# Neighbourhood attention of a one-core hybrid block: scores computed in two layouts, or in one with the exponentials transposed

## The chip, the core and the metric

One core of a Trainium2 chip runs the whole layer in one launch. Time is the device time of that core in microseconds (us). All matrix operands are 32-bit: a product of full precision is written as two or three passes of `float32r` halves (a rounded high part and the remainder as a low part), so most operands exist as a pair `..h`, `..l`.

## The reference

```python
xn = rms_norm(x, norm_g) * (1 + sc_x) + sh_x          # 1024 positions x 1024, modulated by c
cn = rms_norm(ctx, norm_g) * (1 + sc_c) + sh_c        # 256 context positions
f_in, f_gate, q, k, v, na_gate = split(xn @ w_in)     # the context needs only k, v
q, k, kc = rms_norm per head (8 heads of 64)
f_out  = real(fft2(f_in)) @ w_four * silu(f_gate)
s_loc  = where(in window of 8 rows x 16 columns, q.k / 8 + rel_bias, -1e30)
s_ctx  = q.kc / 8                                     # all 256 context keys
p      = softmax(concat(s_loc, s_ctx))                # one softmax over both
na_out = (p_loc @ v + p_ctx @ vc) * silu(na_gate)
out    = x + g_x * (concat(f_out, na_out) @ w_out)
```

Positions are stored by blocks of 8 grid columns, so a block `t` of 128 queries sees keys of the blocks `t-1`, `t`, `t+1` and the two blocks of the context: 512 keys for the first and last block, 640 for the others.

## The kernel before

The layer runs in four stretches. Up to about 140 us: conditioning, norm, the Fourier gate and the Fourier group. From there to about 210 us: Fourier output, projections of the context and the first part of the query, key and value projections. From about 211 us to 538 us: attention, four pairs of heads `p`, two heads `h` in a pair, with projections between its steps. Then the output projection (`of`, L1625).

**Two passes over the scores.** Attention does the following for each head.

- The row pass, `row_max` (L1153), eight times, once for a block `t` of 128 queries: TensorE makes scores `s` with queries on the partitions and keys along the row (L1166, L1168; two passes for the halves). VectorE adds the bias, negates, writes the row to `pr` and takes the row's extreme into `tr` (L1173). ScalarE takes the exponential of `pr` in place, with the extreme as bias, and accumulates the sum of the row (L1177). Of this pass only the extremes and the sums are used: `pr` has two buffers and is overwritten.
- `end_rows` (L1198): one transposition brings extremes and reciprocal sums to eight rows (`pm`). GpSimd spreads the extremes (`spread`, L1188, tile `mrow`) into the free half of the query operand `qs2`, where the ones in `ks2` add them to every score of the second pass, and the reciprocals into `rexp` (two tiles).
- The column pass, `scores` (L1234), twelve steps: TensorE makes the same scores again with keys on the partitions and up to four query blocks side by side (`st`, L1250 and L1251). A step on the window adds a transposed bias on VectorE (`e`, L1259, from `biast`, 448 KB a head) and takes the exponential on ScalarE (L1269). A context step takes it straight from PSUM (L1267). ScalarE rounds `e` to `eh` (L209), and VectorE or GpSimd makes the remainder `el` (L204; GpSimd mostly at context steps). TensorE multiplies both with the values into `pv` (L1282, L1283, L1287).

The pair ends in `finish` (L1296): reciprocals are multiplied into the gate, and the gate into the output.

**What sets the order.** Engines execute in order. Their order is made in Python by a planner: coroutines (`seq_rows`, `seq_scores`, `seq_products` and others) each put out their next piece as soon as the planned clock `now` and the flags in `done` allow it, and each piece on ScalarE, VectorE and GpSimd has a planned duration (`a_t`, `d_t`, `p_t`). When none can go on, `run_fill` puts a product of the projections on TensorE: `pqkv` (L801), `png` (L823) and, in the last pair, the Fourier half of the output projection `po` (L1446). These need nothing from the attention step in progress and are called the filler below. PSUM has one tile `s` of two banks, two tiles `pv0` and `pv1`, two banks for the filler and two (`tb`, counted in `tbs`) that the column pass shares with the transpositions of queries and keys.

## Time and profile before

| what | value |
|---|---|
| median of 3 runs | 602.2 us (601.92 to 603.22) |
| the profiled execution | 599.94 us, its span 598.2 us |
| TensorE busy | 548.5 us, 92% of the span |
| VectorE busy | 468.6 us, 78% |
| ScalarE busy | 354.4 us, 59% |
| GpSimd busy | 222.7 us, 37% |
| chain that ended last, by engine | TensorE 59%, VectorE 24%, ScalarE 6%, issue 5% |

PE is TensorE, PEld its loads of weights, DVE VectorE, ACT ScalarE, POOL GpSimd. "Busy" counts an instruction from start to end. On TensorE matmuls overlap in the pipeline: a matmul over 384 columns lasts 0.34 us in the rows, and the next one starts 0.17 us after it. What a matmul costs is the distance from start to start, called its cadence below.

### The profile page before, as it was taken

The numbers are of one execution on the slowest core, as the hardware profiler recorded it, in microseconds if no ns is written. First come the engines' busy times: TensorE is split into PE (matmuls) and PEld (weight loads), VectorE is DVE, ScalarE is ACT, GpSimd is POOL, SyncE is SP. The second block draws the span as 40 slices with busy tenths as digits, with TensorE's granted clock in tenths as the row PEclk, the third lists the DMA queues.
The fourth block names the chain that finished last, engine by engine and source line by source line (L and its number), as shares of the span: only waits on it lengthen the run. The fifth ranks groups of instructions, "written<-read, shape, count | busy, mean of one in ns | idle before, by whom it ended". The sixth has DMA issues, their size and how long they took to land.

```text
span 598.2 us, 8590 instructions
## 1 busy us (share of the span) xinstructions
PE 548.5 (92%) x2923; PEld 481.6 (81%) x2923; DVE 468.6 (78%) x904; ACT 354.4 (59%) x747; POOL 222.7 (37%) x198
## 2 busy tenths in 40 slices
PE   6799567999999999979999999999999799999997
PEld 4588457989778979979889889799898578787886
DVE  5999999976897787677895878976779959779342
ACT  6865053365633586856877878878677747654100
POOL 3100004015653545342545533444544836424200
PEclk9999958999999999989999999999999898999999
DMA  8970524026783422121032030331104563113152
GB/s 334 407 284 2 175 70 142 2 85 200 260 261 112 149 76 59 43 62 46 22 102 85 22 89 1 111 84 36 50 2 163 163 232 112 66 61 119 35 193 89
DMA packets 42889, 68.83 MB, mean 115 GB/s; under 512 B 3542, under 2 KB 25430, under 8 KB 42844
## 3 DMA queue, kind: packets, MB, share of 16 engines
q1 hardware_dynamic: 41836, 64.60, 32.2%
q0 software_dynamic: 1008, 3.67, 1.8%
q8 instruction: 23, 0.38, 0.3%
q14 instruction: 22, 0.18, 0.1%
HBM read 59.35 MB, written 8.91 MB: 114 GB/s over the span
## 4 chain that ended last, share of the span: by engine, by line
PE 59%; DVE 24%; ACT 6%; issue 5%; DMA 3%; POOL 2%; SPq 1%; DVEq 0%; POOLq 0%; ACTq 0%
PE pqkv L801 16%; PE of L1625 7%; PE pg L369 5%; PE po L1446 5%; PE pv L1287 4%; DVE junk L251 4%; PE png L823 3%; PE st L1250 3%; PE st L1251 3%; PE s L1166 2%; PE s L1168 2%; DVE pr L1173 2%; DVE el L204 2%; DVE l L530 2%; DVE ks L895 1%
## 5 line engine op out<-in xcount | busy, mean ns | idle before, releaser
L801 PE MATMUL pqkv<-wh,xnh 128*128 128x384 f32 x256 | 87.2, 341 | 0.0
L801 PE MATMUL pqkv<-wl,xnh 128*128 128x384 f32 x256 | 87.1, 340 | 0.0
L801 PE MATMUL pqkv<-wh,xnl 128*128 128x384 f32 x256 | 86.8, 339 | 0.0
L1173 DVE CUSTOM_DVE_ANT_0 pr<-s,bias 128x640 f32<-128x640 f32 (+1 forms) x64 | 50.5, 788 | 22.5 <-PE s L1168 16.4
L1177 ACT ACTIVATE pr<-pr,tr 128x640 f32<-128x640 f32 (+1 forms) x64 | 51.4, 803 | 27.4 <-DVE tr L1173 27.2
L707 POOL TENSOR_TENSOR hrs<-hss,mhalf 128x4 f32<-128x4 f32 (+1 forms) x34 | 38.5, 1135 | 65.0 <-DVE hss L704 57.3
L204 DVE TENSOR_TENSOR el<-e,eh 128x384 fp32r<-128x384 f32 (+2 forms) x71 | 50.3, 716 | 12.1 <-ACT eh L209 11.5
L209 ACT CAST eh<-e 128x384 fp32r<-128x384 f32 (+2 forms) x96 | 49.6, 530 | 1.4
L801 PEld LDWEIGHTS pqkv<-wl,xnh 128*128 128x128 f32 x256 | 48.3, 188 | 1.9 <-issue 0.8
L801 PEld LDWEIGHTS pqkv<-wh,xnh 128*128 128x128 f32 x256 | 48.2, 188 | 1.5
L1269 ACT ACTIVATE e<-e 128x384 f32<-128x384 f32 (+1 forms) x64 | 31.6, 497 | 29.6 <-DVE e L1259 29.0
L801 PEld LDWEIGHTS pqkv<-wh,xnl 128*128 128x128 f32 x256 | 48.4, 189 | 0.7
L204 POOL TENSOR_TENSOR el<-e,eh 128x512 fp32r<-128x512 f32 x25 | 32.6, 1302 | 43.4 <-ACT eh L209 43.2
L204 POOL TENSOR_TENSOR wl<-wr,wh 128x384 fp32r<-128x384 f32 (+1 forms) x25 | 31.0, 1244 | 40.6 <-ACT wh L209 26.4
L1259 DVE TENSOR_TENSOR e<-st,biast 128x256 f32<-128x256 f32 (+2 forms) x80 | 34.0, 444 | 8.3 <-PE st L1251 7.7
L1166 PE MATMUL s<-ks,qs 128*128 128x256 f32 (+1 forms) x128 | 30.0, 315 | 8.9 <-DVE tr L1173 8.6
L1166 PEld LDWEIGHTS s<-ks,qs 128*128 128x128 f32 x128 | 23.2, 191 | 16.0 <-DVE tr L1173 13.0
L1250 PE MATMUL st<-qs,ks 128*128 128x512 f32 (+2 forms) x96 | 34.0, 356 | 0.3
L1446 PE MATMUL po<-oh,mh 128*128 128x512 f32 x88 | 32.6, 408 | 0.9 <-DVE gate L829 0.5
L1251 PE MATMUL st<-qs,ks 128*128 128x512 f32 (+2 forms) x96 | 33.5, 349 | 0.0
L369 PE MATMUL pg<-xnh,w 128*128 128x512 f32 x128 | 31.2, 395 | 1.6 <-ACT xnh L360 1.6
L369 PEld LDWEIGHTS pg<-xnh,w 128*128 128x128 f32 x128 | 23.9, 188 | 7.7 <-ACT xnh L360 2.3
(285 smaller groups left out, 1596.8 us busy)
## 6 DMA issues: line engine op xcount, KB each, us to landing
wd<-in_w_ada_t_dram SPq DMA_DIRECT2D x16, 512.0 KB, 8.5
wr<-in_w_in_dram SPq DMA_DIRECT2D x40, 192.0 KB, 2.7
wr<-in_w_in_dram SPq DMA_DIRECT2D x24, 256.0 KB, 3.8
x<-in_xb_dram SPq DMA_DIRECT2D x8, 512.0 KB, 6.9
wdg<-in_w_ada_t_dram SPq DMA_DIRECT2D x8, 512.0 KB, 4.3
owr<-in_w_out_dram SPq DMA_DIRECT2D x16, 256.0 KB, 3.0
y<-in_xb_dram SPq DMA_DIRECT2D x8, 512.0 KB, 5.8
out_dram<-y SPq DMA_DIRECT2D x15, 256.0 KB, 2.1
```

The costliest lines, as they stand in the source:

```text
L204: return [(e, time(n), lambda eng=eng: eng.tensor_tensor(out=out, in0=in0, in1=in1, op=op)) for e, eng, time in (both[k] for k in who)]
L209: return [(e, time(n), lambda cp=cp: cp(out, in_)) for e, cp, time in (both[k] for k in who)]
L369: mm(pg[j][hf], gate_w[i][w][:, j * P:(j + 1) * P], x[i][:, hs], start=(i == 0 and g == 0), stop=(i == KT - 1 and g == 2))
L707: lambda: pool.tensor_tensor(out=rs[:, 0:nh], in0=ss[:, 0:nh], in1=mhalf[:, 0:nh], op=ALU.pow),
L801: mm(o, x[k][:, ts_], w, start=(k == 0 and n == 0), stop=(k == KT - 1 and n == 2))
L1166: mm(o, qs1[h][:, ts_], ks1[h][:, kk], start=st, stop=sp)
L1173: dve.tensor_tensor_reduce(out=pr, in0=sv, in1=bt, scale=-1.0, scalar=3.0e38, op0=ALU.add, op1=ALU.min, accum_out=tr[:, t:t + 1])
L1177: (ACT_, a_t(nl + CTX) + 0.15, lambda: act.activation(pr, pr, AF.Exp, bias=tr[:, t:t + 1], scale=-1.0, accum_out=sm[:, t:t + 1])),
L1250: mm(s, ks1[h][:, kk], qs1[h][:, qq], start=True, stop=False)
L1251: mm(s, ks2[h][:, kk], qs2[h][:, qq], start=False, stop=True)
L1446: mm(o, mf[k][m][:, ts_], wf[hf][k][w_], start=(k == 0 and n == 0), stop=(k == 3 and n == 2))
L1625: mm(o[:, cs], ma[k][m][:, ts_], w[:, cs], start=(k == 0 and n == 0), stop=(k == 3 and n == 2))
```

## The change

- The exponentials of the row pass are kept: five buffers `pr` in place of two (`PRB`), remembered in `prs`.
- The second scores, their bias `biast` with its DMA, their exponentials, the spread of the extremes (`mrow`) and the clearing of its rows go away. Instead a step (`probs`) transposes 128x128 blocks of `pr` on TensorE into the PSUM tile `st`: 16 blocks for the context and 22 for the window per head, 304 in all. ScalarE rounds `st` to `eh`, VectorE subtracts it from `st` to make `el`, always from PSUM, and only then is the bank given back. GpSimd makes no `el` any more.
- Context steps take two query blocks with both context blocks, so their products are 128 of 256 columns instead of 64 of 512.
- `rexp` is one tile of 512 columns, and two selectors `sel` pick its halves.
- Row passes of the next blocks and transpositions of the last ones now stand in one stretch: a step waits for the exponentials of its two or three query blocks, and a row waits until the buffer of the row five before it has been transposed. `EHB`, the number of steps in flight, is 3 instead of 4. The bias has one tile per head of a pair.

```diff
     def build(p):
 
         raw4 = [[("raw", p, t) for t in range(4 * q, 4 * q + 4)] for q in range(2)]
-        prev = [("st", p - 1, 1, 11)] if p else []
+        prev = [("s", p - 1, 1, 7)] if p else []
         yield raw4[0] + prev, True
-        if p:
-            for h in range(2):
-                chain((POOL_, 1.0, lambda h=h: pool.memset(f(qs2[h])[64 - 64 * h:104 - 64 * h], 0.0)),
...
+    PRB, VSB = 5, 1
...
             pool.memset(f(qs2[h])[b], 0.0)
-            pool.memset(f(ks2[h])[b], 1.0)
+            pool.memset(f(ks2[h])[b], 0.0)
...
-        dve.memset(f(mrow), 0.0)
-        rrow = ap1.tile([104, P], R, name="rrow")
...
-            dve.memset(f(sel)[64 * h:64 * h + 40, HALF[h]], 1.0)
-        bias = ap1.tile([P, 896], F32, name="bias")
-        pool.memset(bias[:, 256:512], 0.0)
+        rrow = [ap1.tile([104, P], R, name=f"rrow{n}") for n in range(2)]
+        for r in rrow:
+            dve.memset(f(r), 0.0)
+        half = ap1.tile([104, 2], F32, name="half")
+        sel = [ap1.tile([104, P], R, name=f"sel{z}") for z in range(2)]
+        for z in range(2):
+            dve.reduce_sum(half[:, z:z + 1], eye[:, 4 * z:4 * z + 4], axis=AX.X)
+            dve.memset(f(sel[z]), 0.0)
+            for h in range(2):
...
+                r = slice(64 * h, 64 * h + 40)
+                dve.tensor_copy(sel[z][r, HALF[h]], half[r, z:z + 1].broadcast_to([40, 64]))
+        dve.tensor_tensor(out=eye[:, 0:4], in0=eye[:, 0:4], in1=eye[:, 4:8], op=ALU.add)
+        biases = [ap1.tile([P, 896], F32, name=f"bias{n}") for n in range(2)]
+        for b in biases:
+            pool.memset(b[:, 256:512], 0.0)
         trs = [ap1.tile([P, 40], F32, name=f"tr{h}") for h in range(2)]
         sms = [ap1.tile([P, 8], F32, name=f"sm{h}") for h in range(2)]
         for h in range(2):
...
         hd = 2 * p + h
+        bias = biases[h]
         dma(bias[:, 0:256], bias_ed[hd, 0])
...
                     mm(o, qs2[h][:, ts_], ks2[h][:, kk], start=st, stop=sp)
         now[0] += 2 * (nl + CTX) / 2400
-        pr = ap1.tile([P, 640], F32, tag="pr", bufs=2, name="pr")[:, 0:nl + CTX]
+        done["s", p, h, t] = 1
+        pr = prs[p, h, t] = ap1.tile([P, 640], F32, tag="pr", bufs=PRB, name="pr")[:, 0:nl + CTX]
 
         def top():
             dve.tensor_tensor_reduce(out=pr, in0=sv, in1=bt, scale=-1.0, scalar=3.0e38, op0=ALU.add, op1=ALU.min, accum_out=tr[:, t:t + 1])
             if t == 0:
                 dma(bias[:, 0:256], bias_ed[2 * p + h, 1])
         chain((DVE_, d_t(nl + CTX) + 0.02, top, S["rt"]), lambda: done.__setitem__(("max", p, h, t), 1),
-              (ACT_, a_t(nl + CTX) + 0.15, lambda: act.activation(pr, pr, AF.Exp, bias=tr[:, t:t + 1], scale=-1.0, accum_out=sm[:, t:t + 1])),
+              (ACT_, a_t(nl + CTX) + 0.15, lambda: act.activation(pr, pr, AF.Exp, bias=tr[:, t:t + 1], scale=-1.0, accum_out=sm[:, t:t + 1]), 1),
               lambda: done.__setitem__(("sum", p, h, t), 1))
         if t == NB - 1:
             at(clock() + 1.5, lambda: recip(p, h))
...
 
-    def spread(dst, src, n, t0, t1):
-
-        m, w = t1 - t0, n.stop - n.start
+    def spread(dst, src):
+
         pool.tensor_tensor(
             out=dst.rearrange("p (t n) -> p t n", n=P),
-            in0=f(src)[n].rearrange("p (o n) -> p o n", o=1).broadcast_to([w, m, P]),
-            in1=eye[n, t0:t1].rearrange("p (t o) -> p t o", o=1).broadcast_to([w, m, P]), op=ALU.mult)
+            in0=f(src).rearrange("p (o n) -> p o n", o=1).broadcast_to([104, 4, P]),
+            in1=eye[:, 0:4].rearrange("p (t o) -> p t o", o=1).broadcast_to([104, 4, P]), op=ALU.mult)
...
-        pt = tb("pm")[0:40, 0:P]
-        pe.transpose(pt, tr, ident)
+        pt = tb("pm")[0:8, 0:P]
+        pe.transpose(pt, tr[:, 32:40], ident)
...
+        r0, rr = 64 * h, rrow[p % 2]
+        chain((ACT_, 0.15, lambda: act.copy(rr[r0:r0 + 8], pt)),
+              (DVE_, 0.2, lambda: dve.tensor_tensor(out=rr[r0 + 32:r0 + 40], in0=pt, in1=f(rr[r0:r0 + 8]), op=ALU.subtract)),
...
+        rexp[p] = ap1.tile([104, 512], R, tag="rexp", name="rexp")
+        on([(POOL_, p_t(512), lambda: spread(rexp[p], rrow[p % 2]))], lambda: done.__setitem__(("rexp", p), 1))
...
-    STEPS = ((8, 0, 9, 1, 18, 2, 19, 3, 4, 5, 6, 7), (8, 9, 18, 19, 0, 1, 2, 3, 4, 5, 6, 7))
...
+    STEPS = (10, 11, 0, 1, 2, 3, 12, 4, 13, 5, 6, 7)
+    EHB = 3
+    pvs = {}
...
+    def turned(p, h, t, kt):
+
+        edge = t in (0, NB - 1)
+        if kt < NB:
+            c = (kt - max(t - 1, 0)) * P + (0 if edge else CTX)
         else:
...
+        return prs[p, h, t][:, c:c + P]
+
+    def queries_of(step):
+        return [2 * (step - 10), 2 * (step - 10) + 1] if step > 9 else list(range(max(step - 1, 0), min(step + 2, NB)))
+
+    def last_step(t):
+
+        return STEPS.index(min(t + 1, NB - 1))
+
...
+    def probs(p, h, i):
+        step = STEPS[i]
+        qs = queries_of(step)
...
+        src = [(t, kt) for kt in (8, 9) for t in qs] if step > 9 else [(t, step) for t in qs]
+        n = len(src)
+        w = slice(1, 1 + n) if step == 4 else slice(0, n)
...
-        mm(s, ks1[h][:, kk], qs1[h][:, qq], start=True, stop=False)
-        mm(s, ks2[h][:, kk], qs2[h][:, qq], start=False, stop=True)
-        now[0] += 2 * n * P / 2400
+        for j, (t, kt) in enumerate(src):
+            pe.transpose(s[:, j * P:(j + 1) * P], turned(p, h, t, kt), ident)
+        now[0] += 0.107 * n
...
-            ops = [(ACT_, a_t(m), lambda: act.activation(ew, s3, AF.Exp)), give]
-        else:
-            ops = [(DVE_, d_t(m), add), give, lambda: done.__setitem__(("add", p, h, kt), 1), (ACT_, a_t(m), lambda: act.activation(ew, ew, AF.Exp))]
...
-        ops += [copy_by(m, WHO["ec"], eh[:, w], ew), split_by(m, WHO["ce" if kt >= 8 else "el"], el[:, w], ew, f(eh)[:, w]),
...
+        chain((ACT_, a_t(m), lambda: act.copy(eh[:, w], s3)),
+              (DVE_, d_t(m), lambda: dve.tensor_tensor(out=el[:, w], in0=s3, in1=f(eh)[:, w], op=ALU.subtract)), give,
+              *(((DVE_, 0.27, clear),) if step in (3, 4) else ()),
+              lambda: done.__setitem__(("e", p, h, i), 1), rank=1)
...
+        if step > 9:
+            now[0] += 1024 / 2400
+            z, c = divmod(step - 10, 2)
+            for y in range(2):
+                for x in (eh, el):
+                    mm(pv[z][:, 256 * c:256 * c + 256], vs[:, h, 8 + y], x[:, 2 * y:2 * y + 2], start=(step == 10 and y == 0 and x is eh), stop=False)
...
-            mm(o, sel, rexp[p][hf], start=True, stop=True)
+            mm(o, sel[hf], rexp[p], start=True, stop=True)
...
+        for p, h in HEADS:
+            while p and ("max", p - 1, h, 7) not in done:
+                yield False
+            start_rows(p, h)
+            yield True
...
+    def seq_rows():
...
+                r = 16 * p + 8 * h + t - PRB
+                while r >= 0 and ("st", r // 16, r // 8 % 2, last_step(r % 8)) not in done:
+                    yield False
+                row_max(p, h, t)
+                last = (p, h, t)
                 yield True
...
+    def seq_ends():
+        for p, h in HEADS:
+            while not (("rec", p, h) in done and tbs[0] > 0):
+                yield False
+            end_rows(p, h)
+            yield True
...
+            for i, step in enumerate(STEPS):
+                while not (has(*(("sum", p, h, t) for t in queries_of(step))) and tbs[0] > 0 and len(flow) < EHB):
+                    yield False
...
+                steps.append((p, h, i))
+                g = probs(p, h, i)
...
+                need = [("e", p, h, i), ("v", p, h, 2 if step > 9 else step // 4)]
```

On TensorE, in the first pair, rows of its second head (`s` with `qs_2047`) stand between steps of the first (`st`, `pv`) with filler (`pqkv`) in the gaps. Before:

```order
L1166 MATMUL s<-ks_2051,qs_2047 128x384
L1166 MATMUL s<-ks_2051,qs_2047 128x256
L1168 MATMUL s<-ks_2053,qs_2049 128x384
L1168 MATMUL s<-ks_2053,qs_2049 128x256
L801 MATMUL pqkv<-wl,xnh_351 128x384
L801 MATMUL pqkv<-wh,xnl_355 128x384
L1287 MATMUL pv_2564<-eh,vs 128x256
L1287 MATMUL pv_2564<-el,vs 128x256
L1250 MATMUL st<-qs_2046,ks_2050 128x512
L1251 MATMUL st<-qs_2048,ks_2052 128x512
L1287 MATMUL pv_2564<-eh,vs 128x512
L1287 MATMUL pv_2564<-el,vs 128x512
```

A column step is two products of up to 512 columns. In the change, at the place where the second head's blocks 4 and 5 run (`st<-ident,pr` is a transposition of a kept block):

```order
L1249 MATMUL st<-ident,pr 128x128 x3
L800 MATMUL pqkv<-wh,xnl_122 128x384
L1169 MATMUL s<-ks_2051,qs_2047 128x384
L1169 MATMUL s<-ks_2051,qs_2047 128x256
L1171 MATMUL s<-ks_2053,qs_2049 128x384
L1171 MATMUL s<-ks_2053,qs_2049 128x256
L1283 MATMUL pv_2669<-eh,vs 128x384
L1283 MATMUL pv_2669<-el,vs 128x384
L1249 MATMUL st<-ident,pr 128x128 x4
L800 MATMUL pqkv<-wh,xnh_119 128x384
L800 MATMUL pqkv<-wl,xnh_119 128x384
L800 MATMUL pqkv<-wh,xnl_123 128x384
```

The two products of a step have become three or four transpositions, of blocks that the same head's rows made two or three rows earlier. At the end of the program 130 products `po` stand behind the last `pv`, where 54 stood before.

On VectorE, at the end of the same head, before the change (`e` adds the bias, `el` is the remainder, `mrow` and `rrow` belong to the spread, `raw` and `hss` to the norm of the next projections):

```order
L1263 MEMSET el 128x128
L1264 MEMSET eh 128x128
L1206 TENSOR_TENSOR mrow<-pm,mrow 8x128
L1210 TENSOR_TENSOR rrow<-pm,rrow 8x128
L204 TENSOR_TENSOR el<-e,eh 128x384
L708 TENSOR_TENSOR raw<-raw,hrs 128x256
L204 TENSOR_TENSOR el<-e,eh 128x384
L1263 MEMSET el 128x128
L1264 MEMSET eh 128x128
L1259 TENSOR_TENSOR e<-st,biast 128x256
L1259 TENSOR_TENSOR e<-st,biast 128x128
```

The same head in the change, at its last row:

```order
L1260 TENSOR_TENSOR el<-st,eh 128x384
L702 TENSOR_REDUCE hss<-sqt 128x4
L703 TENSOR_SCALAR hss<-hss 128x4
L1256 MEMSET el 128x128
L1257 MEMSET eh 128x128
L1177 ISA pr,tr_2084<-s,bias_2080 128x512
L1177 ISA tr_2084 128x1
L1260 TENSOR_TENSOR el<-st,eh 128x512
L1260 TENSOR_TENSOR el<-st,eh 128x384
L707 TENSOR_TENSOR raw<-raw,hrs 128x256
L1190 RECIPROCAL tr_2084<-sm_2086 128x8
L1256 MEMSET el 128x128
```

The rows `e` and `mrow` are gone, `el` reads `st` instead of `e`, and the row pass (`ISA pr`) stands among the remainders up to the head's end.

## Rows read from the trace of the kernel before

**Rows 1.** All engines in attention: length, busy us (instructions), PEclk, DMA share, GB/s

```profile
196.00:551.00 355.00, 337.61 (x1820) 303.99 (x1819) 283.26 (x589) 253.68 (x549) 168.57 (x144) 0.99 0.26 81
```

**Rows 2.** Groups by line on PE: count, busy us, mean ns, idle before

```profile
L1250 PE MATMUL st<-qs,ks 128*128 128x384 f32 x48 | 16.4, 341 | 0.0
...
L1250 PE MATMUL st<-qs,ks 128*128 128x512 f32 x32 | 13.0, 407 | 0.1
...
L1250 PE MATMUL st<-qs,ks 128*128 128x256 f32 x16 | 4.8, 302 | 0.2
```

**Rows 3.** Timeline of PE, transpositions of queries and keys: start us, length us

```profile
201.64 0.60 PE L877 MATMUL ptq<-ident,raw 128*128 128x128 f32 x4
202.07 0.60 PE L891 MATMUL ptk<-ident,raw 128*128 128x128 f32 x4
202.43 0.42 PE L801 MATMUL pqkv<-wh,xnh 128*128 128x384 f32 x1
202.69 0.33 PE L801 MATMUL pqkv<-wl,xnh 128*128 128x384 f32 x1
202.86 0.33 PE L801 MATMUL pqkv<-wh,xnl 128*128 128x384 f32 x1
```

**Rows 4.** Timeline of PE in the first pair, both score passes

```profile
251.10 0.39 PE L1250 MATMUL st<-qs,ks 128*128 128x512 f32 x1
...
251.57 0.39 PE L1166 MATMUL s<-ks,qs 128*128 128x256 f32 x2
251.80 0.40 PE L1168 MATMUL s<-ks,qs 128*128 128x256 f32 x2
252.03 0.34 PE L801 MATMUL pqkv<-wh,xnl 128*128 128x384 f32 x1
```

**Rows 5.** Waits of PE in attention: us in total, times, longest

```profile
PE s L1166 <- DVE tr L1173: 8.6, 7, 3.5
PE pv L1282 <- DVE eh L1264: 5.3, 3, 3.1
PE pv L1287 <- DVE el L204: 0.9, 2, 0.5
```

**Rows 6.** Timeline at the first of those waits for eh

```profile
258.57 1.90 POOL L1191 TENSOR_TENSOR qs<-mrow,eye 40x1024 fp32r<-40x1024 f32 x1 [2.04 <-DVE mrow L1206]
...
258.78 2.11 DVE L204 TENSOR_TENSOR el<-e,eh 128x384 fp32r<-128x384 f32 x1
...
263.81 0.43 PE L1282 MATMUL pv<-eh,vs 128*128 128x256 f32 x1 [3.07 <-DVE eh L1264]
```

**Rows 7.** PE in the same stretch: length, busy (count), granted clock, DMA

```profile
259.00:265.00 6.00, 2.93 (x16) 0.91 0.00 0
```

**Rows 8.** The line of the bias sum: duration ns min/median/max, starts, forms

```profile
L1259 DVE TENSOR_TENSOR e<-st,biast x80: 273/425/559, 244.2 to 534.2; 128x256 f32<-128x256 f32 x32, 128x384 f32<-128x384 f32 x32, 128x128 f32<-128x128 f32 x16
```

**Rows 9.** The tile el, its remainder on DVE

```profile
L204 DVE TENSOR_TENSOR el<-e,eh x71: 405/557/2110, 247.2 to 536.6; 128x384 fp32r<-128x384 f32 x48, 128x256 fp32r<-128x256 f32 x16, 128x512 fp32r<-128x512 f32 x7
```

**Rows 10.** Groups by line on DVE in attention

```profile
L1173 DVE CUSTOM_DVE_ANT_0 pr<-s,bias 128x640 f32<-128x640 f32 (+1 forms) x64 | 50.5, 788 | 22.5 <-PE s L1168 16.4 <-ACT pr L1177 3.3 <-ACT eh L209 1.3
L204 DVE TENSOR_TENSOR el<-e,eh 128x384 fp32r<-128x384 f32 (+2 forms) x71 | 50.3, 716 | 12.1 <-ACT eh L209 11.5
```

**Rows 11.** Groups by line on ACT in attention

```profile
L1177 ACT ACTIVATE pr<-pr,tr 128x640 f32<-128x640 f32 (+1 forms) x64 | 51.4, 803 | 27.4 <-DVE tr L1173 27.2
L209 ACT CAST eh<-e 128x384 fp32r<-128x384 f32 (+2 forms) x96 | 49.6, 530 | 1.4
L1269 ACT ACTIVATE e<-e 128x384 f32<-128x384 f32 (+1 forms) x64 | 31.6, 497 | 29.6 <-DVE e L1259 29.0
L1267 ACT ACTIVATE e<-st 128x512 f32<-128x512 f32 x32 | 18.8, 595 | 9.4 <-PE st L1251 9.3
```

**Rows 12.** Groups by line on POOL in attention

```profile
L204 POOL TENSOR_TENSOR el<-e,eh 128x512 fp32r<-128x512 f32 x25 | 32.6, 1302 | 43.4 <-ACT eh L209 43.2
L1191 POOL TENSOR_TENSOR qs<-mrow,eye 40x1024 fp32r<-40x1024 f32 x8 | 15.9, 1990 | 18.6 <-DVE mrow L1206 18.4
```

More of the change, by code (lines that the diff above doesn't have):

```diff
@@ L1477, in seq_build @@
                 yield True
+    HEADS = [(p, h) for p in range(4) for h in range(2)]
     def seq_bias():
@@ new lines, in seq_bias @@
+        for p, h in HEADS:
[4 more added lines that the diff above has]
+    def seq_rows():
+        last = None
+        for p, h in HEADS:
+            while not has(("q", p, h, 0), ("k", p, h, 0), ("k", p, h, 2), ("bias", p, h)):
+                yield False
+            for t in range(NB):
+                while (t > 2 and ("k", p, h, 1) not in done) or (t > 3 and ("q", p, h, 1) not in done) or (last and ("max", *last) not in done):
+                    yield False
+                r = 16 * p + 8 * h + t - PRB
[3 more added lines that the diff above has]
+                last = (p, h, t)
+                yield True
@@ L1510, in seq_rows @@
+    def seq_ends():
+        for p, h in HEADS:
+            while not (("rec", p, h) in done and tbs[0] > 0):
                 yield False
+            end_rows(p, h)
+            yield True
     flow, steps = [], []
     def seq_scores():
-        for p in range(4):
-            for h in range(2):
-                while not (has(("rows", p, h), ("q", p, h, 1), ("k", p, h, 1))):
+        last = None
+        for p, h in HEADS:
+            for i, step in enumerate(STEPS):
+                while not (has(*(("sum", p, h, t) for t in queries_of(step))) and tbs[0] > 0 and len(flow) < EHB):
@@ L1518, in seq_scores @@
                     yield False
[L1519 to L1520 removed]
+                while len(steps) >= S["ns"] and ("e", *steps[-S["ns"]]) not in done:
                     yield False
[L1522 to L1535 removed]
+                steps.append((p, h, i))
@@ L1537, in seq_products @@
+                g = probs(p, h, i)
+                next(g)
+                need = [("e", p, h, i), ("v", p, h, 2 if step > 9 else step // 4)]
+                if last and step in (10, 3):
+                    need.append(("ot", *last, 4 if step == 10 else 7))
+                if p and h == 0 and step == 4:
+                    need.append(("fin", p - 1))
+                flow.append((need, g))
+                yield True
+            last = (p, h)
     def seq_products():
```

134 lines of the change are left out of this document (25 added, 109 removed).

## The prediction

> **What bounds the kernel now.** I read the page's busy table first, then the stretch of attention alone, then the cadence of TensorE's instructions in the timeline, then TensorE's waits, and last the groups of the other engines. The busy table says TensorE, but over the whole span that is an average, so the stretch from 196 to 551 us matters, where everything that the change touches lies. There TensorE is busy 337.6 of 355.0 us, VectorE 283, ScalarE 254, GpSimd 169 [rows 1]. TensorE executes in order, and there is filler to the end, so the length of this stretch is what TensorE has to do plus what it loses.
>
> What it has to do is counted by cadences. A product over 512 columns costs (251.57 - 251.10) / 2 = 0.235 us, one over 256 columns (252.03 - 251.57) / 4 = 0.115 [rows 4], one over 384 columns 202.86 - 202.69 = 0.17. Eight transpositions and one product of 384 fill 201.64 to 202.69, so a transposition costs (1.05 - 0.17) / 8 = 0.11 [rows 3]. With the program's counts: 660 products pqkv at 0.17 are 112; 384 of png and po at 0.235 are 90; the row scores, 96 at 0.17 and 160 at 0.115, are 35; the column scores, 96, 64 and 32 of 384, 512 and 256 columns [rows 2] and each in two passes, are 16.3 + 15.0 + 3.7 = 35; the products pv 37; 72 transpositions 8; small ones 4. Together 321. So some 34 us of the 355 are lost: 17.4 visible as idle time [rows 1], the other half in starts that come later than the cadence but before the last matmul ended.
>
> Whom TensorE waits for: VectorE, each time. The row scores wait 8.6 us for the reduction of the row before, the products pv 5.3 us for cleared halves of eh and 0.9 us for el [rows 5]. The longest wait for eh shows why: while GpSimd spreads extremes for 1.90 us from 258.57, the subtraction el on VectorE, whose usual time is 0.557 us, takes 2.11, and the memset that TensorE waits for stands behind it [rows 6, 9]. In rows 8 the bias sum, which takes one operand from PSUM, never exceeds 0.559 us in 80 times, while el with both operands in SBUF reaches 2.11 [rows 9]. The second source of slowness is therefore GpSimd, not VectorE's own work.
>
> [...]
>
> **The change, part by part.**
>
> *TensorE's work.* Gone: 192 column-score products, 35.0 us by the count above. New: 38 transpositions a head, 304 in all, at 0.11: 33.4 us. Context products: 64 at 0.235 are 15.0, 128 at 0.115 are 14.7. Net -1.9 us, so TensorE has as much to do as before. The bounds of a transposition: 0.11 in a run of eight from below, 0.60 / 4 = 0.15 from above, if no neighbour hid the end of a run of four [rows 3]; that would add 12 us. I take 0.11, because runs of three and four stand between products that hide their ends just as the product at 202.43 starts 0.36 after the last run began.
>
> *VectorE.* Gone: 80 bias sums of mean 0.425, 34.0 us [rows 8]. The remainders: 71 on VectorE took 50.3 [rows 10]; now all 96 stand there, and by rows 8 an operation with one PSUM input takes 0.27 for 128 columns and 0.14 more for each further 128, so 0.42, 0.55 and 0.69: 16 x 0.42 + 48 x 0.55 + 32 x 0.69 = 55. Net -29 us. *ScalarE.* Gone: exponentials of the column pass, 31.6 + 18.8 = 50 us; the 96 roundings stay at 49.6 in all, since from PSUM the 512-wide exponential takes 0.595, no more than from SBUF [rows 11]. *GpSimd.* Gone: 32.6 + 15.9 us [rows 12], the clearing and half of rexp, over 50 us. Beside these the transposed bias goes from the DMA queue; no row shows TensorE waiting for it, so this counts nothing.
>
> *The waits for eh and el.* Their cause leaves: no spread of extremes, no GpSimd remainders, el out of PSUM. [...]
>
> *The row waits, 8.6 us.* They stand where the queries, keys, values and, in the last pair, the output weights of VectorE push in front of a row. None of that is edited: 0. A VectorE with 29 us less could halve them (-4), and the preparation of the selectors, nine small operations more when attention opens, can add up to 2.
>
> *The losses that show no idle time, about 17 us.* They come from steps that arrive a few tenths late. VectorE has a tenth less to do and ScalarE a fifth; I take a fifth of them, -3.4. The bounds are 0 and -17.
>
> *What is added: new waits.* A transposition waits for its row's reduction and exponential: 0.79 [rows 10] + 0.80 [rows 11] and, estimated, 0.4 for reading sums out and hand-overs, 2.0 us. Counting the new order by cadences, TensorE has at least 2.4 us of other work between a row's products and its first transposition (median 4.7), so this is covered, barely in the tightest places. A product pv waits for eh and el of its step: 0.52 + 0.55 + 0.3 = 1.4; between lie at least 1.5 us, median 2.6. Before, the chain had four links (2.4 us) and the order gave it at least 2.7. The bank st is now held until el is done instead of until the bias sum, 1.4 us instead of 0.9; the step after next follows after 1.2 us once, and otherwise after 1.85 or more. Behind a late transposition stands everything on TensorE, filler too. I take +1 us, with bounds 0 and +29 (below).
>
> Sum: -1.9 - 6.7 - 3.4 + 1 = -11. The profiled execution took 599.94 us (1.7 around its span of 598.2), so 588.9 in its terms. The median of the runs is 602.2, 2.3 above that execution: **591 us**. After attention 130 products po instead of 54 follow the last pv; filler only changes place by that, and its 76 products are counted above.
>
> **The rivals.**
>
> *More is freed.* If VectorE's and ScalarE's relief removes half the row waits and three quarters of the hidden losses: -1.9 - 6.7 - 4.3 - 13 = -26, 576 us. For it: every wait of TensorE is for VectorE [rows 5]. Against: the row pass and the remainders of one head now stand together, and in that stretch VectorE and ScalarE still have some nine tenths of TensorE's time to fill.
>
> *The waits move.* The eh waits go, and new ones of the same sum come in the dense stretch: only -1.9 stays, 600 us. For it: a dense stretch is new; against: the distances counted above are all longer than the chains.
>
> *Slower: the shared bank and the dense stretch.* A step needs ScalarE and then VectorE, and a row's reduction (0.79) may stand before either. Of two banks st, one comes free only after both. The slack in the tight places is 0.1 to 0.5 us. As soon as VectorE comes 0.3 us later than the order assumes, a step waits; were that so at all 96 steps, 29 us would be lost, and 602 - 11 + 29 = 620. At two thirds of them it is 610. It decides against the change from some 40 steps on. For it: the plan reckons 0.76 us for a row's reduction, which takes 0.79 and a read-out; against: the same error was in the order before.
>
> *A lower clock.* [...] The kernel would lose a tenth of 240 us of attention if transpositions let it fall to 0.91: 591 + 22 = 613. [...] No run here has shown 304 of them among products; the eight of rows 3 agree with no loss.
>
> **How the numbers follow.** Forecast (584 to 598) 0.50; more freed (568 to 584) 0.20; waits move (598 to 604) 0.13; slower by the dense stretch (604 to 620) 0.11; lower clock 0.06. A measurement of this kernel tells 0.2% from no change, 1.2 us, so "same" is 601.0 to 603.4. Faster: 0.50 + 0.20 + 0.07 of the moving waits, 0.77; same 0.06; slower 0.17. The range leaves out a tenth at either end: 575 to 606.
>
> **What would show it.** Right: 304 transpositions at 0.11 in place of st's products; no el on VectorE above 0.75 us beside GpSimd; no wait of a pv for a cleared eh; row waits about as before; TensorE idle in attention down from 17.4 to some 11 us. Wrong: transpositions that wait for el (the bank) or for pr on ScalarE by many tenths, a PEclk below 0.95 in the slices of attention, or a cadence of 0.15 and more for transpositions.

## The result and the profile after

The changed kernel takes 585.4 us (median of 4 runs, 582.8 to 586.2), the kernel before 602.1 beside it (600.5 to 603.2): a ratio of 0.9717, with a 95% interval of 0.9678 to 0.9756. Forecast were 591 us and a range of 575 to 606. The profiled execution took 586.07 us, its span is 584.3.

The whole gain lies between the first row product and the first product of the last stage. A window of exactly that stretch, of the kernel before and then of the changed one (columns: window, its length, busy time and instructions of each engine, granted clock, DMA share, GB/s):

```profile
211.31:550.56 339.25, 321.86 (x1726) 288.41 (x1725) 270.34 (x561) 244.15 (x530) 158.61 (x133) 0.98 0.25 78
```

```profile
214.35:536.77 322.42, 311.72 (x1902) 287.76 (x1901) 241.60 (x503) 197.83 (x434) 97.48 (x92) 1.00 0.23 73
```

The stretch is 16.8 us shorter. TensorE's idle time in it fell from 17.4 to 10.7 us, VectorE's work by 28.7, ScalarE's by 46.3, GpSimd's by 61.1, and the granted clock went from 0.98 to 1.00. The stretch begins 3.0 us later than before: 2.1 of that was there when the context stage ended, which the change doesn't touch (its last product ends anywhere from 194.0 to 197.7 us in the fourteen profiles of this study). The other 0.9 lies between that product and the first row product; 0.7 of it is a wait of TensorE at 211.78 us, behind VectorE's small operations for the selectors, which last until 209.2 us instead of 205.5. So the span shrank by 13.9 only, and the median by 16.7.

What TensorE waits for in the attention, against [rows 5]:

```profile
PE pv L1273 <- DVE el L1260: 3.0, 4, 1.1
PE po L1445 <- DVE y L1451: 2.0, 3, 1.1
PE s L1169 <- DVE tr L1177: 1.6, 3, 0.7
PE po L1445 <- DVE gate L828: 1.5, 1, 1.5
PE ptq L876 <- DVE raw L707: 1.4, 1, 1.4
```

The waits for the cleared eh are gone. New ones for el stand at the context steps, 3.0 us. The row waits, which were to stay, fell from 8.6 to 1.6 us. No wait is longer than 1.5 us.

The longest wait for el, 1.12 us, shows that one thing has not gone with the change:

```profile
456.19 2.39 POOL L203 TENSOR_TENSOR ml<-omr,mh 128x1024 fp32r<-128x1024 f32 x1 [1.60 <-ACT mh L208]
456.34 2.39 DVE L203 TENSOR_TENSOR vs<-ckp,vs 128x128 fp32r<-128x128 f32 x1
459.38 0.38 PE L1273 MATMUL pv<-el,vs 128*128 128x256 f32 x1 [1.12 <-DVE el L1260]
```

The remainder vs on VectorE, 128 columns from two operands in SBUF, takes 2.39 us beside a GpSimd operation of 1024 columns; at 453.05 us the same operation takes 0.38. The el that TensorE waits for stands behind it. Two of the other three waits (0.35 and 0.45 us) stand behind wl (the low part of a weight), which takes 1.34 us beside GpSimd's own wl, and 0.54 without it.

el, against [rows 9], by shortest, median and longest:

```profile
L1260 DVE TENSOR_TENSOR el<-st,eh x96: 407/554/694, 229.4 to 502.7; 128x384 fp32r<-128x384 f32 x48, 128x512 fp32r<-128x512 f32 x32, 128x256 fp32r<-128x256 f32 x16
```

With one operand from PSUM no el is longer than 0.694 us, where 2.11 stood. All 96 on VectorE cost 53.3 us; 55 were forecast.

The transpositions, against [rows 3] (a piece of the timeline: start, length of the group, engine, line, operation, names, shape, count):

```profile
258.99 0.34 PE L1283 MATMUL pv<-el,vs 128*128 128x384 f32 x1
259.17 0.60 PE L1249 MATMUL st<-ident,pr 128*128 128x128 f32 x4
259.52 0.42 PE L800 MATMUL pqkv<-wh,xnh 128*128 128x384 f32 x1
259.78 0.34 PE L800 MATMUL pqkv<-wl,xnh 128*128 128x384 f32 x1
```

Four transpositions and a product of 384 columns fill 259.17 to 259.78; less 0.17 for the product that is 0.44, 0.11 each. They neither wait (0.0 us of idle time ahead of all 304) nor lower the clock, which stays at 1.00.

The clock is what the waits don't show. In the kernel before there are exactly three stretches at half clock (a granted clock of 0.50) in the attention, each 3.41 us long; windows laid on them:

```profile
263.95:267.36 3.41, 3.41 (x13) 3.40 (x14) 2.67 (x8) 2.25 (x5) 1.01 (x1) 0.50 0.20 23
472.16:475.57 3.41, 2.92 (x9) 2.14 (x9) 3.41 (x7) 2.54 (x5) 2.42 (x2) 0.50 0.71 282
496.06:499.47 3.41, 3.41 (x11) 2.93 (x10) 2.83 (x6) 2.89 (x8) 2.40 (x2) 0.50 0.92 329
```

Each begins 0.1 to 1.3 us after one of the long waits has ended (at 263.81, 471.93 and 494.73 us), and the second is seen in the timeline of the kernel before, too:

```profile
471.93 0.72 PE L1166 MATMUL s<-ks,qs 128*128 128x384 f32 x2 [3.51 <-DVE tr L1173]
...
474.69 0.63 PE L1446 MATMUL po<-oh,ml 128*128 128x512 f32 x1
475.11 0.61 PE L1446 MATMUL po<-oh,mh 128*128 128x512 f32 x1
...
476.38 0.39 PE L1446 MATMUL po<-oh,ml 128*128 128x512 f32 x1
476.61 0.39 PE L1446 MATMUL po<-oh,mh 128*128 128x512 f32 x1
```

After TensorE has stood for 3.51 us a product of 512 columns takes 0.42 us from start to start; at 476.38 it is back at 0.23. Half the clock for 3 x 3.41 us loses up to 5.1 us of work (TensorE was busy in all but 0.49 us of the 10.23). The changed kernel has no such stretch in its attention.

The last of the three follows a row wait of 1.93 us. What VectorE does ahead of it, before the change and then at the same operations after it:

```profile
492.39 1.27 POOL L204 TENSOR_TENSOR ol<-owr,oh 128x512 fp32r<-128x512 f32 x1
492.46 1.47 DVE L209 CAST oh<-owr 128x512 fp32r<-128x512 f32 x1 [1.19 <-POOL owr L1359]
493.86 0.81 DVE L1173 CUSTOM_DVE_ANT_0 pr<-s,bias 128x640 f32<-128x640 f32 x1
494.73 0.56 PE L1166 MATMUL s<-ks,qs 128*128 128x384 f32 x2 [1.93 <-DVE tr L1173]
```

```profile
488.90 0.43 DVE L208 CAST oh<-owr 128x512 fp32r<-128x512 f32 x1 [1.37 <-POOL owr L1358]
```

Beside GpSimd's subtraction the rounding of oh takes 1.47 us, with GpSimd idle 0.43; the row behind it, one operation later, then waits 0.41 us. Ahead of the longest row wait (3.51 us) VectorE's queue is long (ks, ol, qs and two vs between 467.27 and 471.0), and the operation ahead of these, a remainder ml of 1024 columns, had taken 2.59 us beside GpSimd's ml.

### The profile page after: what moved, and what is told of

Read it like the earlier page. It is cut to its first block, busy times and chain, and to the rows that moved or that the text cites. A ratio compares the mean times of both kernels' runs of the same rounds, so it can differ in the third digit from the quotient of the medians.

```text
span 584.3 us, 8657 instructions
## 1 busy us (share of the span) xinstructions
PE 540.9 (93%) x3099; PEld 483.4 (83%) x3099; DVE 436.1 (75%) x847; ACT 304.8 (52%) x646; POOL 155.2 (27%) x153
## 4 chain that ended last, share of the span: by engine, by line
PE 56%; DVE 24%; ACT 8%; DMA 5%; issue 4%; POOL 2%; SPq 0%; DVEq 0%; ACTq 0%; POOLq 0%
PE pqkv L800 17%; PE of L1621 7%; PE pg L368 5%; PE st L1249 4%; DVE junk L250 4%; PE po L1445 4%; PE s L1169 2%; PE s L1171 2%; PE png L822 2%; PE pv L1283 2%; PE pv L1273 2%; DVE l L529 2%; DMA wr<-in_w_in_dram 2%; DVE s L523 1%; DMA owr<-in_w_out_dram 1%
## 5 line engine op out<-in xcount | busy, mean ns | idle before, releaser
L1260 DVE TENSOR_TENSOR el<-st,eh 128x512 fp32r<-128x512 f32 (+2 forms) x96 | 53.3, 571 | 17.9 <-ACT eh L1259 17.3
L1259 ACT CAST eh<-st 128x512 fp32r<-128x512 f32 (+2 forms) x96 | 46.7, 494 | 32.2 <-PE st L1249 27.3
L1177 DVE CUSTOM_DVE_ANT_0 pr<-s,bias 128x640 f32<-128x640 f32 (+1 forms) x64 | 50.3, 786 | 13.3 <-PE s L1171 12.8
L1249 PE MATMUL st<-ident,pr 128*128 128x128 f32 x304 | 47.1, 272 | 0.0
L1249 PEld LDWEIGHTS st<-ident,pr 128*128 128x128 f32 x304 | 37.1, 140 | 2.3
L1625 DVE TENSOR_TENSOR y<-y,of 128x512 f32<-128x512 f32 (+1 forms) x17 | 11.1, 656 | 32.3 <-PE of L1621 32.3
L1445 PE MATMUL po<-oh,mh 128*128 128x512 f32 x88 | 31.1, 398 | 3.4 <-DVE y L1451 2.0
L1169 PE MATMUL s<-ks,qs 128*128 128x256 f32 (+1 forms) x128 | 29.9, 314 | 1.6 <-DVE tr L1177 1.6
L208 ACT CAST wh<-wr 128x384 fp32r<-128x384 f32 (+1 forms) x46 | 24.2, 544 | 13.6 <-DMA wr<-in_w_in_dram 10.1
L1171 PE MATMUL s<-ks,qs 128*128 128x256 f32 (+1 forms) x128 | 28.6, 303 | 1.1 <-DVE ks L894 1.1
L707 DVE TENSOR_TENSOR raw<-raw,hrs 128x256 f32<-128x256 f32 x32 | 18.2, 576 | 10.8 <-POOL hrs L706 10.7
```

The costliest lines, as they stand in the source:

```text
L1169: mm(o, qs1[h][:, ts_], ks1[h][:, kk], start=st, stop=sp)
L1171: mm(o, qs2[h][:, ts_], ks2[h][:, kk], start=st, stop=sp)
L1177: dve.tensor_tensor_reduce(out=pr, in0=sv, in1=bt, scale=-1.0, scalar=3.0e38, op0=ALU.add, op1=ALU.min, accum_out=tr[:, t:t + 1])
L1249: pe.transpose(s[:, j * P:(j + 1) * P], turned(p, h, t, kt), ident)
L1259: chain((ACT_, a_t(m), lambda: act.copy(eh[:, w], s3)), (DVE_, d_t(m), lambda: dve.tensor_tensor(out=el[:, w], in0=s3, in1=f(eh)[:, w], op ...
L1260: (DVE_, d_t(m), lambda: dve.tensor_tensor(out=el[:, w], in0=s3, in1=f(eh)[:, w], op=ALU.subtract)), give,
```

## The experiments

Twelve kernels ran; the loads put back are work that the layer doesn't need, near the place where the old work stood. The order of TensorE's instructions is that of the changed kernel in all six that put back load or change where el reads from, and that of the kernel before in the run with its spreads on VectorE. The kernel before, run beside them, came to 601.2 to 602.7 us, and a ratio is known to some 0.2 to 0.4%: differences of 2 us between two of these medians are not clear of noise. Each profile is of one execution. For each, the stretch from the first row product to the last stage was taken apart as above: idle is its length less TensorE's busy time, "half clock" is half the length of the stretches at 0.50.

| kernel | median us | ratio to the kernel before (95%) | stretch | idle | half clock |
|---|---|---|---|---|---|
| before | 602.1 | 1 | 339.3 | 17.4 | 5.1 |
| changed | 585.4 | 0.9717 (0.9678 to 0.9756) | 322.4 | 10.7 | 0 |
| transpositions twice | 612.5 | 1.0181 (1.0144 to 1.0218) | 350.6 | 7.3 | 0 |
| GpSimd's load back | 587.1 | 0.9753 (0.9716 to 0.9790) | 326.3 | 12.0 | 3.4 |
| VectorE's load back | 592.9 | 0.9845 (0.9812 to 0.9879) | 330.3 | 12.5 | 1.7 |
| ScalarE's load back | 588.9 | 0.9782 (0.9752 to 0.9812) | 324.5 | 11.6 | 0 |
| all three back | 597.4 | 0.9921 (0.9892 to 0.9951) | 335.5 | 16.1 | 3.4 |
| el from SBUF | 586.6 | 0.9738 (0.9703 to 0.9773) | 325.4 | 12.0 | 1.7 |
| el from SBUF, GpSimd's load back | 604.0 | 1.0041 (1.0013 to 1.0070) | 341.9 | 22.5 | 3.4 |
| before, spreads on VectorE | 600.8 | 0.9982 (0.9959 to 1.0005) | 339.3 | 17.9 | 3.4 |
| late set-up | 583.4 | 0.9683 (0.9651 to 0.9716) | 317.1 | 8.2 | 0 |
| four row buffers | 583.2 | 0.9681 (0.9646 to 0.9715) | 321.0 | 8.8 | 0 |
| late set-up, copies to ScalarE | 585.2 | 0.9702 (0.9667 to 0.9736) | 319.1 | 9.5 | 0 |
| late set-up, four row buffers | 584.1 | 0.9694 (0.9658 to 0.9730) | 319.0 | 9.1 | 0 |

**Transpositions twice.**

```diff
             pe.transpose(s[:, j * P:(j + 1) * P], turned(p, h, t, kt), ident)
+            pe.transpose(s[:, j * P:(j + 1) * P], turned(p, h, t, kt), ident)
```

Expected: 

> The changed kernel with each of its 304 transpositions of the exponentials issued twice, to the same place; the order of all else is unchanged. If TensorE's own work sets the pace and the clock does not mind transpositions: 304 x 0.110 = 33.4 us more work, of which the 11.4 us that TensorE still idles between 196 and 537 us can take a part, so +24 to +33, 610 to 619 us, at a granted clock of 1.00. If instead the chain of each step (turn, copy, subtract, product) sets the pace, the second turn mostly fills idle time: under +15. If transpositions did lower the clock, doubling them would show it: granted clock under 0.95 in the attention and more than +40.

Measured 612.5, +27: of 33.4 us of work, 28.2 lengthen the stretch and 3.4 go into idle time. So TensorE's own work sets the pace of the changed kernel, and with 608 transpositions the clock stays at 1.00. The rival of a lower clock is refuted: 304 and 608 of them among products both left it at 1.00 in the stretch.

**GpSimd's load back.**

```diff
+            if step > 9 and scr:
+                pool.tensor_tensor(out=scr[0], in0=idb, in1=idb, op=ALU.subtract)
             dve.tensor_tensor(out=o, in0=a, in1=b, op=ALU.subtract)
...
+        for _ in range(2 if scr else 0):
+            pool.tensor_tensor(out=scr[0][0:40], in0=idb[0:40], in1=idb[0:40], op=ALU.subtract)
```

Expected: 

> The changed kernel with most of GpSimd's old load put back as work that nothing reads: 29 subtractions of 128x512 from SBUF, beside the context steps, and 16 of 40x512 ahead of the reciprocals' rows, some 54 of the 62 us that GpSimd lost; the order of all other instructions is unchanged. Theory G (GpSimd's long operations had held up VectorE's two-operand reads of SBUF, and through them both the el waits and the row waits): the row waits rise from 1.6 us by 3 or more, raw (two SBUF operands) rises from its mean of 521 ns, el, which now reads one operand from PSUM, stays under 0.75; the time rises by 3 to 7 us. Theory L (it is VectorE's shorter queue): waits stay within 1.5 us of those of the changed kernel and the time within 2.

Measured 587.1, +1.7, within the noise. el stays below 0.7 us (0.693 at the longest) and raw goes from 521 to 529 ns only, against theory G; the row waits rise to 3.3 us and two stretches at half clock come back, which theory L doesn't have. The stretch is 3.9 us longer, but it begins 2.5 us earlier with the context stage: alone this load is worth little.

**VectorE's load back.**

```diff
             dve.tensor_tensor(out=o, in0=a, in1=b, op=ALU.subtract)
+            if step < 10:
+                dve.reduce_sum(scr[1][:, 0:3], scr[0], axis=AX.X)
```

Expected: 

> The changed kernel with VectorE's old load put back: 64 reductions of 128x384, one behind each subtraction of a window step, about 0.41 us each, 26 us in all, against the 28 us by which VectorE's attention had become lighter; order otherwise unchanged. Theory L (the row waits had gone because VectorE's queue is shorter): s waits for tr 5 us or more instead of 1.6, the time +5 to +10. Theory O (the new order, which runs rows up to five buffers ahead and puts steps between them, hides the row pass): row waits under 3 us, time +0 to +3.

Measured 592.9, +7.6. The reductions took 0.54 us each, 34.6 in their own rows; they overlap their neighbours, so VectorE's busy time in the stretch rises by 24.6 us (241.6 to 266.2), where the change had taken 28.7. Theory L had the time right and the place wrong: the row waits stay at 1.2 us.

```profile
PE pv L1282 <- DVE el L1264: 3.5, 4, 1.5
PE po L1454 <- DVE gate L828: 1.9, 1, 1.9
PE po L1454 <- DVE y L1460: 1.5, 2, 1.1
PE ptq L876 <- DVE raw L707: 1.4, 1, 1.4
PE s L1173 <- DVE tr L1181: 1.2, 3, 0.7
```

The named waits hardly differ from the changed kernel's. Of the stretch's +7.8 only 1.8 is idle time and 1.7 the clock; the other 4.3 are in no view of waits (starts a few tenths late, by exclusion).

**ScalarE's load back.**

```diff
             act.copy(o, a)
+            if scr:
+                act.copy(scr[0][:, 0:n], idb[:, 0:n])
```

Expected: 

> The changed kernel with ScalarE's old load put back: 93 copies of ident, as wide as the step, one behind each copy of eh, some 42 us, against the 45 us by which ScalarE had become lighter; order otherwise unchanged. If ScalarE's second pass over the scores had held up the steps (a part of the lost time that the waits do not name), the time rises by 3 to 6 us and el or pr waits appear; if ScalarE, half empty, never mattered: within 2 us.

The copies land in the buffer of the context's raw keys and values, part of which is rounded after them, so some values of the context are others. They took 49.7 us in their own rows and raise ScalarE's busy time in the stretch by 35.8 (197.8 to 233.6). That costs 3.5 us, within the first expectation and hardly clear of noise, and less per microsecond of busy time (3.5 / 35.8 = 0.10) than VectorE's load (7.6 / 24.6 = 0.31).

**All three back.** The loads of the last three together, ScalarE's and GpSimd's in pieces of 256 columns.

Expected: 

> The changed kernel with the three loads of the earlier runs put back together: VectorE's 64 reductions, ScalarE's copies (90 of 128x256, some 35 us) and GpSimd's subtractions (the same amount in pieces of 256 columns). If the gain beyond TensorE's own work and the named waits is the relief of the three engines, and the three add up: from the first row product to the last stage +14 (7.8, 2.1 and 3.9 by the profiles), so 597 to 601 us, nearly the kernel before. If they cover for each other (one engine sets each stall, the others wait beside it): +8 to +10, 592 to 595. In either case the row waits tell how far the order alone keeps them away: under 4 us if the order does it, 6 or more if the load did.

Measured 597.4, +12.0: within the noise the three add up (1.7 + 7.6 + 3.5 = 12.8). 4.0 of the 7.0 us of row waits come back with them:

```profile
PE s L1176 <- DVE tr L1184: 5.6, 6, 2.9
PE pv L1295 <- DVE el L1277: 3.9, 5, 1.6
```

The longest has the same place as the longest of before, the beginning of the last pair, and the timeline shows what VectorE and GpSimd do ahead of it:

```profile
464.49 4.68 DVE L203 TENSOR_TENSOR vs<-raw,vs 128x256 fp32r<-128x256 f32 x4
...
464.52 2.96 POOL L1380 TENSOR_TENSOR owr<-owr,grow 128x512 f32<-128x512 f32 x2
...
467.44 1.44 POOL L203 TENSOR_TENSOR ol<-owr,oh 128x512 fp32r<-128x512 f32 x1
469.09 0.81 DVE L1184 CUSTOM_DVE_ANT_0 pr<-s,bias 128x640 f32<-128x640 f32 x1
...
469.96 0.90 PE L1176 MATMUL s<-ks,qs 128*128 128x384 f32 x2 [2.88 <-DVE tr L1184]
```

Four subtractions for vs, both operands in SBUF, take 4.68 us beside three such operations of GpSimd. The row's reduction stands behind them, and TensorE behind the reduction. A stretch of 6.83 us at half clock begins within the wait, at 469.23. The three GpSimd operations are the kernel's own; what the load does is to shift them. With GpSimd's load alone it is the same:

```profile
457.51 4.82 DVE L203 TENSOR_TENSOR vs<-raw,vs 128x256 fp32r<-128x256 f32 x4
463.12 0.55 PE L1175 MATMUL s<-ks,qs 128*128 128x384 f32 x2 [2.55 <-DVE tr L1183]
```

In the seven kernels with this order on TensorE the four vs last 1.42 us where nothing of GpSimd stands beside them (el from SBUF; no row wait behind), 2.08 to 2.67 beside one or two of its operations (0.42 us at most; 2.67 and 0.42 in the changed kernel), and 4.68 to 4.82 beside three (GpSimd's load alone, all three loads, and el from SBUF with GpSimd's load: waits of 2.55, 2.88 and 1.93). So the new order alone doesn't keep row waits away: the longest of them comes and goes with what GpSimd does beside vs.

**el from SBUF,** without and with GpSimd's load.

```diff
-              (DVE_, d_t(m), lambda: dve.tensor_tensor(out=el[:, w], in0=s3, in1=f(eh)[:, w], op=ALU.subtract)), give,
+              (DVE_, d_t(m), lambda: dve.tensor_tensor(out=el[:, w], in0=idn[:, w], in1=f(eh)[:, w], op=ALU.subtract)), give,
```

Expected without: 

> The changed kernel with el computed from two operands in SBUF (ident in place of the turned exponentials, so what the products take from el is another number), without any load put back: the control for the run that had both and came to 604.0. Theory G (it is GpSimd's work beside a two-operand read of SBUF that costs): GpSimd's remaining 107 us already slow some of the el, mean 600 to 680 ns against 571, longest above 1.2 us; +3 to +8 over the changed kernel, 588 to 594, so that the two together (17 to 19) are more than the parts (1.7 for the load alone and this). Rival (two SBUF operands cost the same with GpSimd's load or without, for another reason than GpSimd): +14 to +17, 600 or more, by this run alone. Third (el from SBUF costs nothing without the load, since two SBUF operands are read quicker, 0.41 for 128x384 where PSUM's take 0.55): within 2 of 585.4.

Expected with: 

> The changed kernel with GpSimd's old load put back as in the run with GpSimd's load, and with el computed from two operands in SBUF (ident in place of the turned exponentials, so that what the products take from el is another number) as the kernel before had it; order unchanged, the shared bank free earlier if anything. Theory G (contention bites where VectorE reads two operands from SBUF): el's longest rises from 0.7 to above 1.2 us, waits of the products for el or eh reach 6 us or more against 3.9, and the time is 3 to 6 us above that of the run with GpSimd's load alone. Rival (where el reads from does not matter): within 2 us of that run.

Measured 586.6 and 604.0. Where el reads costs 1.2 us, GpSimd's load costs 1.7, neither clear of noise, and both together cost 18.6: the rival is refuted in both runs. Without the load the time fits the third expectation, though not by its reason (a remainder of 384 columns takes 0.61 us on the average out of SBUF, 0.55 out of PSUM; in the kernel before most of 256 columns took 0.41 to 0.43, most of 384 took 0.55 to 0.56); with it, theory G's 3 to 6 us over GpSimd's load alone came to 16.9. VectorE's el in the three runs (busy us, mean ns), GpSimd's load alone, el from SBUF alone, both:

```profile
L1270 DVE TENSOR_TENSOR el<-st,eh 128x512 fp32r<-128x512 f32 (+2 forms) x96 | 53.5, 572 | 17.8 <-ACT eh L1272 17.2
```

```profile
L1261 DVE TENSOR_TENSOR el<-ident,eh 128x512 fp32r<-128x512 f32 (+2 forms) x96 | 59.4, 635 | 17.4 <-ACT eh L1260 16.8
```

```profile
L1270 DVE TENSOR_TENSOR el<-ident,eh 128x512 fp32r<-128x512 f32 (+2 forms) x96 | 73.7, 783 | 14.9 <-ACT eh L1272 14.3
L707 DVE TENSOR_TENSOR raw<-raw,hrs 128x256 f32<-128x256 f32 x29 | 18.0, 629 | 9.7 <-POOL hrs L706 9.7
```

With one input in PSUM the load leaves el at 572 ns; with two in SBUF it brings el to 783, and raw, which has always had two, to 629. The vs of 2.39 us in the changed kernel's own profile is the same thing without any load: it stands in the run with both, too (2.40 us, 0.37 elsewhere). VectorE is about as busy in the stretch with both (268.9 us) as with all three loads (271.3), yet here the time is 6.6 us longer. That is theory G.

**Before, spreads on VectorE.**

```diff
-        pool.tensor_tensor(
+        dve.tensor_tensor(
             out=dst.rearrange("p (t n) -> p t n", n=P),
```

Expected: 

> The kernel before, with its 16 spreads (8 of 40x1024, 8 of 104x512) issued on VectorE instead of GpSimd, at the same place of the program; all else is in the same order. Theory G (el was held up beside GpSimd's spreads: 2.11 us where 0.56 is usual): el stays under 0.8 us, the three waits of the products for the cleared eh (5.3 us) and those for el (0.9) mostly go, and the time falls by 3 to 6 us although VectorE is given some 14 us more. Theory L (VectorE's queue as such is what is short): the added 14 us on VectorE cost 3 to 8 us, and the waits for eh stay.

Measured a ratio of 0.9982 (0.9959 to 1.0005): no difference. Neither theory had it; the longest el falls from 2.11 to 1.60 us only.

```profile
PE s L1166 <- DVE tr L1173: 11.8, 11, 5.1
PE pv L1282 <- DVE eh L1264: 1.8, 2, 1.0
PE pv L1283 <- DVE eh L1264: 1.5, 2, 0.7
PE pv L1287 <- DVE el L204: 1.3, 4, 0.4
```

The mean el falls from 716 to 626 ns and the waits for eh from 5.3 to 3.3 us, the longest from 3.07 to 1.0; but the spreads give VectorE 15.2 us, and the row waits rise from 8.6 to 11.8. Taking these operations from GpSimd frees as much as putting them on VectorE costs. The change drops them and pays neither.

**Late set-up.** The selectors and their like are built behind the second row.

```diff
-        free[DVE_] = max(free[DVE_], now[0]) + OD
...
                 row_max(p, h, t)
                 last = (p, h, t)
+                if (p, h, t) == (0, 0, LS):
+                    on([(DVE_, 3.5, set_up)], None, 2)
```

Expected: 

> The changed kernel with the small constants of the attention (eye, half, the selectors, the zeros of rrow: some 5.9 us of VectorE ahead of the first rows) built behind the second row of the first pair, where nothing needs them for 20 us; the planner orders the work around it anew. If VectorE's set-up holds up the first rows (the first row product comes 3.0 us later than before), the first row product comes 1.5 to 4 us earlier and the time falls by 1.5 to 4, 581.5 to 584. Rival (the start is set by the context stage, whose products end 2.1 us later in the changed kernel's profile by chance, and by ks): within 1 us of 585.4.

Measured 583.4. The stretch is 5.3 us shorter, but the first row product comes 3.0 us later: 1.1 with the context stage, and 1.8 since the planner put twelve more filler products png ahead of it. The wait of 0.7 us ahead of the first rows is gone, which speaks for the selectors as its cause. Against the changed kernel the intervals overlap; the expectation isn't decided.

**Four row buffers.**

```diff
-    PRB, VSB = 5, 1
+    PRB, VSB = 4, 1
```

Expected: 

> The changed kernel with four buffers for a row's exponentials instead of five, so that the row pass runs one row less far ahead of the steps (the planner orders the work anew; four is the least with which the order of the steps can run). Theory O (the lead of the rows is what took the row waits away): s waits for tr or TensorE idles beside st for 5 us more than in the changed kernel, the time +4 to +8. Rival (the lead does not matter, the shorter queue of VectorE does): within 2 us of 585.4.

Measured 583.2, row waits 0.7 us; one transposition waits 1.5 us for an exponential. One row of lead less brings no row waits back, against theory O; a lead shorter than four can't be had in this order of steps.

**Late set-up, copies to ScalarE.**

```diff
-WHO = dict(..., q2=(0,), kb=(0, 2), ..., oc=(0, 2), ...)
+WHO = dict(..., q2=(2,), kb=(2,), ..., oc=(2,), ...)
```

Expected: 

> The run with the late set-up, with 25 copies more taken from VectorE and given to ScalarE: the 16 of the second queries (0.47 us each), the 7 of keys and 2 of the output weights that the planner had given to VectorE, some 13 us. From the runs with load put back, a microsecond on VectorE costs 0.3 us and one on ScalarE 0.05: -3 to -4 for VectorE, +1 for ScalarE, so 580 to 581.5 against 583.4. If the copies lie where VectorE has slack, or ScalarE's longer chains (copy behind copy for queries and keys) delay the first rows of each head: 583 to 587.

Measured 585.2. VectorE has 8.2 us less in the stretch, ScalarE 12.0 more, and nothing is gained. Whether these copies lay where VectorE has slack or ScalarE's longer chains took the gain back isn't decided.

**Late set-up, four row buffers.** Both edits.

Expected: 

> The changed kernel with both edits that measured a little below it, four buffers for a row's exponentials (583.2) and the late set-up (583.4, against 585.4). If they act at different places (the one on the waits of the products for el, the other on the first 15 us of the attention), both add: 580.5 to 582. If either only moved the planner's order by luck: 583 to 586. It also shows which of the two the first row product follows.

Measured 584.1: they don't add. Three versions measure 1 to 2 us below the changed kernel, none of them outside its interval, so no better version is shown.

## Why the prediction was right, and which terms were off

The forecast was 588.9 us in the profile's terms, and the profiled execution took 586.1. Behind that stand two misses: the stretch lost 16.8 us where 11 were forecast, and it began 3.0 us later, 2.1 of that by chance. Term by term:

| term | predicted | measured |
|---|---|---|
| TensorE's work | -1.9 | -1.9 (counts of both traces by the prediction's cadences; 0.11 for a transposition measured again) |
| waits for eh and el | -6.2 | -6.2 (none of those of before is left) |
| granted clock | -0.5 | -5.1 |
| row waits | 0 | -7.0 |
| new waits | +1 | +6.5 (3.0 for el, 3.5 of what else there is of idle time: 10.7 - 17.4 + 6.2 + 7.0 = 6.5) |
| losses that show no idle time | -3.4 | -3.1 (what is left) |

- **TensorE's work** was right, and by it so was the point that the change trades scores for transpositions at no gain. The run with transpositions twice shows that this work is what the time now follows.
- **Waits for eh and el.** The -6.7 of the sum is these 5.3 + 0.9 us [rows 5] and 0.5 for the clock, 0.91 over 6.00 us [rows 7]. The mechanism was right: it takes GpSimd's load and an el from SBUF (604.0 us, el 783 ns), and either one's absence is enough (587.1 us with 572 ns, 586.6 with 635).
- **New waits** were sized too small. No wait stands ahead of a transposition, on which the prediction's slower rival rested. A product pv does wait for el at the context steps, 3.0 us, mostly behind a vs or wl that GpSimd slows (2.39 us against 0.38, 1.34 against 0.54); the other 3.5 are short waits for VectorE's y, gate, raw and ks.
- **Row waits**, put at 0 because "none of that is edited", are the step that failed. What is edited is VectorE's queue and what GpSimd does beside it. In the same order of TensorE the waits are 1.2 us with VectorE's load back, 3.3 with GpSimd's, 4.7 with GpSimd's and el from SBUF, 5.6 with all three; the longest of the last three runs stood behind vs, which GpSimd held up (4.68 to 4.82 us for four in those runs, 1.42 with nothing of GpSimd beside them): the same cause as that of the waits for eh, one operation further back. The other 3.0 of the 8.6 come back in none of these runs; whether the new order took them stays open.
- **Granted clock.** The prediction read 0.91 over the window from 259 to 265 us [rows 7] and counted the loss inside it. The slow stretch began at 263.95 and went on to 267.36, behind the window's end, and two more stood behind row waits that it hadn't looked at. Two of the three so belong to the row waits, which makes that term -10.4 in all.
- **Losses without idle time** came out as sized, but only since the clock, part of those 17, is counted apart; together they fell by 8.2.
- **Set-up**, allowed up to 2 us, cost 0.9. The rivals in which the change stays without gain, is slower or lowers the clock did not come. The rival in which more is freed was nearer in kind: it had the row waits halved.
- **Luck.** TensorE's idle time was to fall to some 11 us and fell to 10.7, but by other waits than forecast: 7.0 us less of row waits, 5.5 more of new ones. In the same way the sum is off by 5.8 us only because the misses partly cancel.
- **A small slip.** The 0.425 us that the prediction calls the mean of a bias sum is the median [rows 8]; the 80 sums took 35.5 us instead of 34.0. VectorE's sum is no term of the forecast.

Open stays how the gain divides between the lighter engines and the contention. The loads put back with el out of PSUM account for 12 us, contention on el with GpSimd's load for 18.6, and the whole gain is 16.7: the two overlap, and the runs don't split them.

## What to carry to other kernels

When an engine that is waited for gets lighter, every wait for it is in question, the ones in unedited code too (here the row waits, 8.6 to 1.6 us); look at what stands ahead of them in its queue, and at what GpSimd does at that time. Look for the granted clock past the end of each long wait, not only inside it (here 0.50 for 3.41 us behind three of them). Before moving work off GpSimd or off VectorE, look whether the slow operation reads two operands from SBUF: reading one of them from PSUM bought as much here (604.0 to 587.1 us) as taking the load away (604.0 to 586.6).

## What the runs showed of the hardware that was not expected

- Three waits of 1.9 to 3.5 us in the kernel before were each followed by a stretch of 3.41 us at a granted clock of 0.50, which lost up to another 1.7 us. The length of the wait doesn't settle it: 2.1 us of idle time ahead of po, with ScalarE's load back, left none. What does is not shown.
- A load can cost without being waited for: VectorE's cost 7.6 us with 1.8 us more of idle time.
- Two causes that are worth 1.2 and 1.7 us alone, no more than noise, are worth 18.6 together.
- A rounding with one operand in SBUF is slowed beside GpSimd as well: oh took 1.47 us there, 0.43 alone.
